# A two-layer hybrid decoder step: sample states by one product of three parts, conv states turned four at a time, and four smaller edits

## The chip, the cores and the metric

The kernel runs on one core of a Trainium2 chip. The metric is device time in microseconds (us); the time before is the median of 3 runs. The core has four engines that compute, each with its own queue: TensorE (PE in the profile, with its weight loads as PEld), VectorE (DVE), ScalarE (ACT) and GpSimd (POOL). SyncE (SP) issues the DMA transfers. PE's results go to PSUM, which has eight banks of 512 fp32 columns; everything else works from SBUF.

## The reference

One inference step of two layers, run for a prompt (512 tokens) and for 8 sample sequences of 8 new tokens, 576 tokens in all, with shared weights and a model width of 1024. Layer 0 has a pooling mixer (trailing means over 2, 4, 8 and 16 positions), layer 1 a gated DeltaNet mixer; each is followed by a SwiGLU FFN of width 2816, with an RMS norm before and after each part:

```
for i in range(DEPTH):
    h = rms_norm(x, norm_mix_pre[i])
    m = pool_mixer(h, ...) if i % 2 == 0 else gdn_mixer(h, ...)
    x = x + rms_norm(m, norm_mix_post[i])
    h = rms_norm(x, norm_ffn_pre[i])
    x = x + rms_norm(swiglu(h, ffn_w_in[i], ffn_w_out[i]), norm_ffn_post[i])
```

The DeltaNet mixer projects to q, k (8 heads of 128), v and a gate z (16 heads of 128), runs a causal convolution of width 4 over q, k and v, and then a recurrence per head on a state S of 128 x 128: S_t = a_t S_{t-1} + k_t (beta_t (v_t - a_t S_{t-1}^T k_t))^T, with output S_t^T q_t. The reference does it in chunks. Inputs and outputs also hold states: the last 15 pooling rows, the last 3 rows before the convolution (for each sample sequence and for the prompt, 4096 channels), and S itself for each sample sequence and head.

## The kernel before

**Numbers.** Operands of the large products are split into a rounded part and a remainder in a fast fp32 form (F32R): `split2` (line 1002) and `Weights.split` (981) make them with one ACT copy and one subtraction on DVE or POOL. `mm3` (990) then makes three products of each block: high x high, high x low, low x high. Small products are in plain fp32, and each of those leaves two records in the trace.

**Stages.** Activations lie with channels on partitions and tokens along columns, in two halves of 256 and 320 tokens (`HALVES`; the second holds the 64 sample tokens). First the pooling mixer and layer 0's FFN (lines 1224 to 1405), then the DeltaNet layer in four groups of two key heads and four value heads (`project`, `core`, `zgate`, lines 1523 to 2104), then the rest of its output product, and layer 1's FFN (2107 to 2199).

**FFN.** `ffn` (1098) has 22 column blocks, each a pair of a gate block and an up block. The first `head` pairs (`HEADS` = 7 in layer 0, 5 in layer 1, line 33) are made by `plain` (1125): for each half of the tokens it loads both weights and makes 24 products each, first all pairs of the first half, then all of the second. The others are made by `seven` (1144), which makes seven products of quarter blocks, of 288 columns each, in place of eight; it needs combinations of the weights (four half-size additions and subtractions on DVE or POOL) and of the activations (`twist`, 1085), and so both halves of the tokens.

**Norms.** `add_sq` (1011) squares each of the eight channel blocks on ACT and adds them into `nacc`, all but the last, which stays apart as a second addend `nsq`. `rstd` (1032) then sums over partitions by products of one column with a vector of ones, one for each addend and each 128 tokens; `finish1` (2177) does the same at the very end.

**Conv states.** `project` loads the 24 rows of earlier states (8 sequences x 3) as `crow`, 24 x 4 x 128, and turns each 128 channels by a transpose on PE (1548 to 1556); at the end (1652 to 1662) it turns the new rows `nct` back, 27 x 128 at a time (8 x 3 and the prompt's 3), copies them with ACT and stores them.

**Sample states.** `sample_front` (1694) prepares the keys of the 64 sample tokens: `ks` holds the rounded keys in rows 0 to 63 and their remainders in rows 64 to 127. `sample_heads` (1758) runs for each key head while the prompt's `scan` (1826) goes on. It loads the states of the 8 sequences, spreads `ks` into `km`, one block per sequence in which the other sequences' rows are zero, and updates each state by two products in one sum, with `vH` (the rounded values, in both row halves) and with `vL` (their remainders):

```
for bb in range(2):
    PE.matmul(pS[:, bb], km[:, b + bb], vH, start=True, stop=False)
    PE.matmul(pS[:, bb], km[:, b + bb], vL, start=False, stop=True)
```

Two smaller products per head use 64 rows of the array: `Ts` with `rs` (1794) and `Qs` with `vn` (1804, at a tile position).

**Order.** Nothing is issued as it is written. `Plan` (336) records all instructions, with costs per engine (`cost`, 434) and with the dependencies between them, and places them by a model of the engines (`forward`, 640). What is ready on an engine goes by rank; the table `MOVES` (line 53, 1405 entries) is a list of seeds that stir the ranks of stretches of instructions, one after the other. An instruction put on `EITHER` goes to DVE or POOL, one on `BOTH` to DVE or ACT, whichever the planner finds; where PE would stand idle long enough, it puts in products that nobody reads (`ps_w`). Buffers are rings of fixed size: three raw weight blocks, three split ones, and PSUM banks by name ("s": banks 0 to 2, "k": 6 and 5, "x": 7, `RING`, line 908).

Of the kernel before, what the change touches and what calls it, by code (L numbers as in the profile page):

```python
# [32 lines left out]
HEADS = (7, 5)  # L33
# [20 lines left out]
1.1d7anak.0.rf.u7 1.y2f47l.2s.0.bvc 1.s0vq82.2s.0.ti 1.pp743b.0.0.bvc 1.4z4ke2.0.9qg.a1k 0.au7bb7.2s.7t9.bo5  # L54
0.1frtbjm.2s.5sa.5v2 0.ee6mun.rs.39q.4fe 0.7sepyh.2bc.7i2.7t6 0.bbjoxv.rs.913.93v 0.8wxv3b.rs.3y7.40z
0.tf6kvk.rs.8tp.8wh 0.wyvqlx.2s.2to.3zc 0.bh9a6p.2bc.7q0.814 0.8hwl7j.2bc.816.8ca 0.jlysq9.8c.31x.47l
0.1nsdy99.8c.4iq.4tu 0.9yytj2.rs.27i.2im 0.igs0if.rs.9vd.b11 0.jxqs1k.rs.9jq.9uu 0.vegd0o.2s.0.3c0
0.1b0k30b.8c.9t0.9vs 0.pjwnuj.8c.hp.st 0.1643rle.rs.9wv.9zn 0.1urop5.2bc.73d.765 0.19ues0m.2bc.als.aok
0.67m20i.8c.71r.7cv 0.llkt9y.rs.6jb.6m3 0.bvvr7t.rs.7t7.84b 0.1q3ehmt.8c.23s.2ew 0.1qgeil4.2s.9ce.ai2
0.y8xkqt.8c.8x7.a2v 0.aoy0ng.rs.2pu.2sm 0.1fkb0ee.2bc.4c5.4ex 0.t07ml0.2bc.bmg.bvc 0.1xjj1qh.2s.9uj.9xb  # L60
0.1uf81p2.8c.6az.6dr 0.1d8z5m7.rs.2ch.2nl 0.1nsjl6j.2s.8kv.8vz 0.15jg0om.rs.89w.8co 0.hs4389.rs.anj.aqb
0.171qk9e.rs.7z4.81w 0.1140n12.2s.8hs.9ng 0.1azm7gz.2s.3ax.3m1 0.vijnsy.2bc.bss.bvc 0.10hprob.rs.1me.2s2
0.wi7odi.8c.89w.8co 0.dfvamo.2bc.aqa.at2 0.3jc2jj.8c.2e2.2gu 0.ps4ghp.2bc.56q.5hu 0.1r0ffal.2bc.8ya.912
0.xfacbh.2s.781.8dp 0.1fp5dk3.2bc.3ok.3zo 0.1slwoeh.2bc.70z.86n 0.1vgjcmy.2s.82h.985 0.1gi4m9f.2bc.4hm.4ke
0.87h1q0.rs.54h.5fl 0.rfnq0w.8c.8ql.bvc 0.q4hmzs.8c.9sc.a3g 0.10nufsc.2s.0.1q5 0.1tiapdn.2s.b6l.bvc
0.17t45od.rs.4a9.855 0.5rdedg.rs.9tc.9w4 0.1j4zh0k.2bc.6e.96 0.1ss67k0.rs.a6f.ahj 0.2svvgn.8c.agj.ajb
0.bpoomp.rs.bpu.bsm 0.t3o181.2bc.41f.4cj 0.1wv9twd.2s.1ck.57g 0.1tf1mpa.8c.od.1u1 0.69rvzm.2bc.9fe.9qi
0.1pj35r4.rs.9r8.9u0 0.1ce0uqr.8c.2um.40a 0.gjfyk0.8c.0.6p 0.46rblf.2s.3gc.3rg 0.14ty5f3.2s.8u9.9zx
# [12 lines left out]
0.a7ikvn.2s.6mv.6pn 0.1bygjfd.2s.bnt.bvc 0.1koaur1.rs.8pn.90r 0.1wf7dro.rs.98t.9jx 0.ji5ev1.rs.a90.ak4
0.1yp3jqj.rs.bfn.bif 0.1jv2yn6.rs.5vg.5y8 0.1mws14w.8c.8bp.9hd 0.i1evgw.2s.4gk.4jc 0.e2qeak.2bc.bb5.bm9
0.11gd8un.rs.92n.95f 0.1favvlm.8c.1fj.1ib 1.3ktxmq.0.7cu.7fm 0.177ynii.rs.9pq.ave 0.1r5eqxe.8c.33t.3ex
0.ma35m2.rs.1d5.2it 0.lymuvx.8c.2td.34h 0.1x8yzja.2s.a8.454 0.muxcdo.8c.8sl.8vd 0.14uzngk.2s.5gn.6mb
0.n0a1h5.8c.3t.3yp 0.1vmszuc.2s.36d.3hh 0.1kk9pm2.rs.7dk.7oo 0.17owqc0.2s.b0l.bvc 0.1cw9cxp.2bc.9n4.9y8
0.elx6d7.8c.5in.6ob 0.1dkpzq2.2bc.86x.89p 0.9mpa4v.8c.5dp.5ot 0.jijbp0.2bc.b6h.bhl 0.x120r.2s.7cw.8ik
0.2qokrq.rs.9ax.agl 0.ap74jx.rs.50w.5c0 0.1qf2ph5.rs.7w9.7z1 0.w56vte.rs.7ba.7e2 0.msgyjb.rs.6yq.84e
0.psozk2.2bc.8p9.8s1 0.6ru0ma.2bc.aag.alk 0.1ilo347.2s.8nn.bvc 0.yqg8b1.2s.a62.a8u 0.1mz5fg.8c.9ek.ak8
0.6lrs3y.8c.37r.3iv 0.4ffzsh.2s.9u8.a5c 0.kn8378.2bc.7w5.879 0.12kjhdl.rs.brk.buc 0.1gh7g5c.2s.7xy.892
0.18rvxdw.2s.5kq.5vu 0.1o2vxzq.2s.abg.bh4 0.17lajt1.2s.37i.3im 0.wyvpxk.8c.ss.13w 0.3czbgp.8c.4gk.4ro  # L90
0.1qng8px.2s.9wc.9z4 0.sobty9.2s.ahw.bvc 0.bi7va.2bc.335.3e9 0.1djjjua.2s.8rp.92t 0.1bvnacn.8c.vx.21l
0.171wwzd.8c.6ju.6uy 0.14u3rt5.rs.aqt.b1x 0.q50eg2.8c.9c7.ahv 0.vs1jfk.8c.bo5.bvc 0.1e1loh1.rs.7e1.7p5
0.1tmmbse.2s.9cm.9fe 0.nnoxbq.2s.b8o.bvc 0.n6n6h.2s.b8l.bvc 0.1o8bli5.8c.a52.a7u 0.bqy70q.2bc.b6l.bhp
0.isq8m3.rs.9ih.ao5 0.1274coh.2s.7is.8og 0.1b57b2j.8c.9m6.9xa 0.16oa8wk.2s.8ka.8n2 0.3w8q6h.rs.asp.b3t
0.1jutx9e.rs.b00.bb4 0.2zogkx.8c.6xh.709 0.1yuo622.rs.9pl.a0p 0.1ub0xk.2s.7ok.7zo 0.tki80c.2bc.7as.7dk
0.1ipjkno.2s.6sf.7y3 0.vhdfhd.rs.beg.bvc 0.mjbrxi.2bc.bcc.bf4 0.106vtjh.2bc.bjk.bmc 0.vomtm9.rs.9t3.a47
0.gggz5r.rs.bd9.bg1 0.v2xi33.8c.6n0.6y4 0.f42swr.2bc.70f.863 0.1qq27nd.8c.9ks.aqg 0.j464d9.rs.7w7.87b
0.1yozlmv.8c.bhg.bsk 0.5ntm1d.2bc.7cp.7nt 0.udmov4.2bc.8ug.8x8 0.ojoyjb.8c.9p9.aux 0.frz7ky.8c.7lc.7o4
0.l8y1qd.2s.98o.aec 0.ihecg0.8c.bef.bvc 0.1xadojx.2s.b7f.bvc 0.191175k.8c.agp.art 0.1u1nu8d.2s.60b.9v7
0.190c9ra.2s.581.6dp 0.ta4nji.rs.7pk.7sc 0.1hwnhjy.8c.aog.ar8 0.1nyltl2.2bc.5bk.5ec 0.1grqjg2.2s.9v6.b0u  # L100
0.3itv7y.8c.3lk.3oc 0.18rqmv.2bc.3k7.3mz 0.1i3b1pf.2bc.8ym.91e 0.h5wypn.2bc.bid.bl5 0.16uivga.8c.1gv.2mj
0.116d6uj.8c.aoc.azg 0.18ki0vc.2bc.bp0.brs 0.1es7bvt.rs.bse.bvc 0.2byfdo.8c.b7i.bim 0.4fyhs.2bc.bnt.bvc
0.h4jgec.8c.7ch.7nl 0.nhn8vl.2s.6yu.84i 0.1tp9pgh.2bc.858.8gc 0.18enz4u.2s.bab.bvc 0.1sg6l91.rs.bga.bvc
0.1hqzskx.rs.9ya.b3y 0.s3xg4v.8c.7o7.7qz 0.asw9he.2s.9d6.9oa 0.pvi32f.rs.9h3.9jv 0.1s43nou.8c.5h.89 0.zwcxin.2s.0.236
# [231 lines left out]
class Plan:  # L336
# [303 lines left out]
    def forward(self, rank):  # L640
# [65 lines left out]
        while todo:  # L706
# [1525 lines left out]
```

## Time and profile before

| what | before |
|---|---|
| time, median of 3 runs | 1530.03 us (1528.61 to 1533.35) |
| profiled execution, its time | 1528.16 us |
| its span, first to last instruction | 1526.4 us |
| PE busy | 1505.5 us (99%), 11856 records |
| PE weight loads busy | 1454.6 us (95%) |
| DVE busy | 1152.9 us (76%) |
| ACT busy | 835.7 us (55%) |
| POOL busy | 116.8 us (8%) |
| DMA | 198.91 MB, mean 130 GB/s |

Nearly all instructions stand at one line of the kernel (582, where the plan issues them), so groups are read by their tiles: "ps_s<-vL,km" is a product into a bank of ring "s" with `km` as weights and `vL` moving. Records of products overlap, since PE starts one before the last has left the array; a group's mean duration is therefore longer than the spacing between its products. Three DVE operations and more stand at lines 812 and 817, ACT's at 826, 829 and 835: these are the ones that the planner chose between the two engines.

### The profile page before, as it was taken

The numbers are of one execution on the slowest core, as the hardware profiler recorded it, in microseconds if no ns is written. First come the engines' busy times: TensorE is split into PE (matmuls) and PEld (weight loads), VectorE is DVE, ScalarE is ACT, GpSimd is POOL, SyncE is SP. The second block draws the span as 40 slices with busy tenths as digits, with TensorE's granted clock in tenths as the row PEclk, the third lists the DMA queues.
The fourth block names the chain that finished last, engine by engine and source line by source line (L and its number), as shares of the span: only waits on it lengthen the run. The fifth ranks groups of instructions, "written<-read, shape, count | busy, mean of one in ns | idle before, by whom it ended". The sixth has DMA issues, their size and how long they took to land. (4 is left out here: it accounts for less than half of the span.)

```text
span 1526.4 us, 30360 instructions
## 1 busy us (share of the span) xinstructions
PE 1505.5 (99%) x11856; PEld 1454.6 (95%) x11856; DVE 1152.9 (76%) x2323; ACT 835.7 (55%) x1765; POOL 116.8 (8%) x259
## 2 busy tenths in 40 slices
PE   8999999999999999999999999999999999999998
PEld 7999999999999999899899889989999999999998
DVE  5996358658788698997898799567799637837865
ACT  7764334324465975874874784746565334414455
POOL 4210000000012010110120010100110000000000
PEclk9999999999999999999999999999999999999999
DMA  6364323322476433434533443666865432332363
GB/s 190 110 188 138 99 82 97 99 82 84 135 224 184 130 103 100 113 103 123 145 100 102 126 123 111 199 177 190 244 207 157 113 88 66 94 101 70 102 190 124
DMA packets 350358, 198.91 MB, mean 130 GB/s; under 512 B 13963, under 2 KB 344364, under 8 KB 350207
## 3 DMA queue, kind: packets, MB, share of 16 engines
q1 hardware_dynamic: 350215, 196.97, 45.0%
q8 instruction: 93, 1.52, 0.4%
q14 instruction: 50, 0.41, 0.1%
HBM read 166.65 MB, written 30.52 MB: 129 GB/s over the span
## 5 line engine op out<-in xcount | busy, mean ns | idle before, releaser
L582 DVE TENSOR_TENSOR wl<-wraw,wh 128x1024 fp32r<-128x1024 f32 (+1 forms) x224 | 267.1, 1200 | 103.2 <-ACT wh L582 75.2
L582 ACT ACTIVATE wh<-wraw 128x1024 fp32r<-128x1024 f32 (+1 forms) x227 | 232.4, 1030 | 195.6 <-PE ps_A L582 70.7
L582 PE MATMUL ps_m<-hH,wh 128*128 128x256 f32 (+1 forms) x832 | 246.4, 309 | 0.0
L582 PE MATMUL ps_m<-hL,wh 128*128 128x320 f32 (+1 forms) x832 | 246.4, 308 | 0.0
L582 PE MATMUL ps_m<-hH,wl 128*128 128x256 f32 (+1 forms) x832 | 244.9, 307 | 0.0
L582 PEld LDWEIGHTS ps_m<-hH,wh 128*128 128x128 f32 x832 | 154.3, 189 | 2.8 <-issue 0.6
L582 PEld LDWEIGHTS ps_m<-hL,wh 128*128 128x128 f32 x832 | 154.6, 189 | 2.5 <-issue 0.5
L582 PEld LDWEIGHTS ps_m<-hH,wl 128*128 128x128 f32 x832 | 154.3, 190 | 2.4 <-issue 0.6
L582 PE MATMUL ps_B<-hH,wh 128*128 128x320 f32 (+1 forms) x392 | 114.8, 304 | 0.0
L582 PE MATMUL ps_B<-hL,wh 128*128 128x320 f32 (+1 forms) x392 | 114.0, 305 | 0.0
L582 PE MATMUL ps_B<-hH,wl 128*128 128x320 f32 (+1 forms) x392 | 113.2, 305 | 0.0
L582 PE MATMUL ps_B<-aH,wh 128*128 128x320 f32 x352 | 105.5, 311 | 0.6 <-ACT wh L582 0.6
L582 PE MATMUL ps_B<-aH,wl 128*128 128x320 f32 x352 | 105.8, 312 | 0.0
L582 PE MATMUL ps_A<-hH,wh 128*128 128x256 f32 (+1 forms) x376 | 104.7, 290 | 0.1
L582 PE MATMUL ps_B<-aL,wh 128*128 128x320 f32 x352 | 104.7, 310 | 0.0
L582 PE MATMUL ps_A<-hL,wh 128*128 128x256 f32 (+1 forms) x376 | 104.3, 288 | 0.0
L582 PE MATMUL ps_A<-hH,wl 128*128 128x256 f32 (+1 forms) x376 | 103.0, 288 | 0.0
L582 PE MATMUL ps_A<-aH,wl 128*128 128x256 f32 x352 | 94.6, 281 | 0.0
L582 PE MATMUL ps_A<-aL,wh 128*128 128x256 f32 x352 | 94.6, 281 | 0.0
L582 PE MATMUL ps_A<-aH,wh 128*128 128x256 f32 x352 | 94.4, 282 | 0.0
L582 DVE SCALAR_TENSOR_TENSOR ac<-u,cwt,ac 128x600 f32<-128x600 f32 x96 | 79.9, 844 | 2.5 <-ACT ac L582 2.1
L582 PEld LDWEIGHTS ps_B<-hH,wh 128*128 128x128 f32 x392 | 72.7, 188 | 0.1
(462 smaller groups left out, 4175.9 us busy)
## 6 DMA issues: line engine op xcount, KB each, us to landing
wraw<-in_ffn_w_in_dram SPq DMA_DIRECT2D x112, 512.0 KB
wraw<-in_gdn_w_in_dram SPq DMA_DIRECT2D x56, 512.0 KB
wraw<-in_ffn_w_out_dram SPq DMA_DIRECT2D x48, 448.0 KB
wraw<-in_gdn_w_out_dram SPq DMA_DIRECT2D x24, 512.0 KB
wraw<-in_ffn_w_out_dram SPq DMA_DIRECT2D x16, 512.0 KB
St<-in_state_gdn_rec_dram SPq DMA_DIRECT2D x32, 256.0 KB
out_dram<-St SPq DMA_DIRECT2D x32, 256.0 KB
z_d<-zz SPq DMA_DIRECT2D x16, 288.0 KB
```

The costliest lines, as they stand in the source:

```text
L582: calls[e](*a, **k)
```

## The change

- Layer 0's FFN has 6 plain pairs in place of 7; one more pair is made by `seven`.
- Sample states: four sequences' tokens are 32 rows. `ks` and `vHL` are laid out so that one product of 128 rows holds three parts of 32 rows each, rounded keys with rounded values, rounded keys with the values' remainders, and the keys' remainders with rounded values; the fourth quarter is zero. There are two such layouts, for sequences 0 to 3 and 4 to 7. The remainders' own product, which was in the sum before, is left out. `km` is made in two halves with a new mask, `seqm4`.
- The products with `Ts` and `Qs` run over all 128 rows, with zeros (memsets on POOL) in the rows that don't count; `vn` is needed in the upper rows alone and may go to DVE or ACT.
- Conv states are loaded and stored with four channel blocks under each other on partitions (96 rows in, 108 out), so that one transpose turns four; each block has its own transfers.
- `add_sq` adds the last square to the sum, except in layer 0's mixer norms (`apart`).
- The planner's model: a POOL copy costs 137 ns more; an instruction on an engine other than PE that touches a PSUM bank waits in the model for the bank's last user on another engine than PE; and `MOVES` is a new table of 574 entries.

```
-HEADS = (7, 5)
+HEADS = (6, 5)
...
-                t = 0.85 * n + (100 if method == "memset" else 183)
+                t = 0.85 * n + (100 if method == "memset" else 320)
...
+            late = max((quiet[x] + self.LAT[e] - t for x in ops[i][10] if user.get(x, e) not in (e, "PE")), default=0.0)
+            if e != "PE" and late > 0.0:
+                hold, done = hold + late, done + late
...
-            if c == NC - 1:
+            if c == NC - 1 and apart:
                 acc.append(sq)
...
-                crow = pp.tile([R0, 4, P], F32, name="crow", tag="nco", bufs=1)
+                crow = pp.tile([4 * R0, P], F32, name="crow", tag="nco", bufs=1)
                 for j, i0, n in pc:
...
-                for j in range(4):
-                    PE.transpose(cp[:, 4 * j4 + j], crow[:, j], ident[:R0, :R0])
-            ACT.activation(cst_t.rearrange("p c b r -> p c (b r)"), cp, AF.Copy)
+                    for i in range(n):
+                        SP.dma_start(crow[(j + i) * R0:(j + i + 1) * R0],
+                                     state_gdn_conv[0].rearrange("b r d -> (b r) d")[:, (i0 + i) * P:(i0 + i + 1) * P])
+                PE.transpose(cp[:, 4 * j4 * R0:4 * (j4 + 1) * R0], crow, ident[:4 * R0, :4 * R0])
+            ACT.activation(cst_t.rearrange("p c b r -> p (c b r)"), cp, AF.Copy)
...
-                for j in range(4):
-                    PE.transpose(pn_[:R, j], nct[:, 4 * j4 + j], ident)
-                ACT.activation(nco, pn_[:R], AF.Copy)
+                nco = pp.tile([4 * R, P], F32, name="nco", tag="nco", bufs=1)
+                pn_ = bank("x")[:4 * R, :P]
+                PE.transpose(pn_, nct[:, 4 * j4:4 * j4 + 4].rearrange("p c r -> p (c r)"), ident)
+                BOTH.move(nco, pn_)
...
-                ACT.activation(ks[:, hd], pt, AF.Copy)
-                DVE.tensor_tensor(ks[E2[1], hd], pt[E2[1]], ks[E2[1], hd].bitcast(F32), op=sub)
+                for x_ in range(2):
+                    BOTH.move(ks[:, hd, x_], pt)
+                for x_ in range(2):
+                    a, b, c = (slice(32 * q, 32 * q + 32) for q in (x_, 1 - x_, 2 + x_))
+                    BOTH.move(ks[b, hd, x_], pt[a])
+                    DVE.tensor_tensor(ks[c, hd, x_], pt[c], ks[c, hd, x_].bitcast(F32), op=sub)
...
-                EITHER.tensor_tensor(km, ks[:, hd:hd + 1].bitcast(F32).to_broadcast([P, NB, P]),
-                                   seqm2.unsqueeze(2).to_broadcast([P, NB, P]), op=mult)
+                for x_ in range(2):
+                    b4 = slice(4 * x_, 4 * x_ + 4)
+                    EITHER.tensor_tensor(km[:, b4], ks[:, hd, x_:x_ + 1].bitcast(F32).to_broadcast([P, 4, P]),
+                                         seqm4[:, b4].unsqueeze(2).to_broadcast([P, 4, P]), op=mult)
...
-                    PE.matmul(pv[:, 0, e * P:(e + 1) * P], Ts[:, hd, e], rs[:, e], start=True, stop=True)
...
+                    PE.matmul(pv[:, 0, e * P:(e + 1) * P], TQ[:, hd, e], sn[:, 0, e], start=True, stop=True)
+                BOTH.scaled(vn, pv[up, 0].rearrange("p (e v) -> p e v", e=2), bet[up, SPANS, h2])
...
-                split2(ve, vH, vL)
+                vHL = cp_.tile([P, 2, 2, P], F32R, name="vHL", tag="vHL", bufs=1)
+                for x_ in range(2):
+                    BOTH.move(vHL[:, x_], ve)
+                for x_ in range(2):
+                    a, b = (slice(32 * q, 32 * q + 32) for q in (x_, 1 - x_))
+                    EITHER.tensor_tensor(vHL[b, x_], ve[a], vHL[a, x_].bitcast(F32), op=sub)
...
-                    PE.matmul(po[up, 0, e * P:(e + 1) * P], Qs[:, hd, e], vn[up, e], start=True, stop=True,
-                              tile_position=(SMP, SMP))
+                    PE.matmul(po[:, 0, e * P:(e + 1) * P], TQ[:, hd, e], sn[:, 2, e], start=True, stop=True)
...
-                        PE.matmul(pS[:, bb], km[:, b + bb], vH, start=True, stop=False)
-                        PE.matmul(pS[:, bb], km[:, b + bb], vL, start=False, stop=True)
+                        PE.matmul(pS[:, bb], km[:, b + bb], vHL[:, b // 4], start=True, stop=True)
```

More of the change, by code (lines that the diff above doesn't have):

```diff
@@ L59 @@
[L59 to L68, printed above, removed]
@@ L656, in forward @@
         still = {name: len(h) for name, h in self.holds.items()}
-        quiet = {}
+        quiet, user = {}, {}
         def note(t, work):
@@ L782, in forward @@
                 quiet[name] = max(quiet.get(name, 0.0), end)
+                user[name] = e
             for j in succ[i]:
@@ L892, in hybrid_kernel @@
     seqm = seqm2[:SMP]
+    seqm4 = cst.tile([P, NB], F32, name="seqm4")
+    for q in range(4):
+        sm = seqm4[32 * q:32 * q + 32].rearrange("p (x b) -> p x b", x=2)
+        POOL.affine_select(sm, ones[:32, :NB].rearrange("p (x b) -> p x b", x=2), [[0, 2], [-NT, NB // 2]], ALU.is_ge, 0.0,
+                           base=0, channel_multiplier=1)
+        POOL.affine_select(sm, sm, [[0, 2], [NT, NB // 2]], ALU.is_ge, 0.0, base=NT - 1, channel_multiplier=-1)
+    POOL.memset(seqm4[64:96, 4:], 0.0)
+    POOL.memset(seqm4[96:, :4], 0.0)
     prm = cst.tile([P, 73], F32, name="prm")
@@ L1654, in project @@
             for j4, pc in enumerate(pieces):
-                nco = pp.tile([R, 4, P], F32, name="nco", tag="nco", bufs=1)
-                pn_ = bank("x", (P, 4, P))
-                for j in range(4):
-                    PE.transpose(pn_[:R, j], nct[:, 4 * j4 + j], ident)
-                ACT.activation(nco, pn_[:R], AF.Copy)
+                nco = pp.tile([4 * R, P], F32, name="nco", tag="nco", bufs=1)
+                pn_ = bank("x")[:4 * R, :P]
+                PE.transpose(pn_, nct[:, 4 * j4:4 * j4 + 4].rearrange("p c r -> p (c r)"), ident)
+                BOTH.move(nco, pn_)
                 for j, i0, n in pc:
-                    src = nco[:, j:j + n].rearrange("r c p -> r (c p)")
-                    SP.dma_start(nc_prompt[0, 0, :, i0 * P:(i0 + n) * P], src[:CW - 1])
-                    SP.dma_start(nc_sample[0].rearrange("b r d -> (b r) d")[:, i0 * P:(i0 + n) * P], src[CW - 1:])
+                    for i in range(n):
+                        src, cols = nco[(j + i) * R:(j + i + 1) * R], slice((i0 + i) * P, (i0 + i + 1) * P)
+                        SP.dma_start(nc_prompt[0, 0, :, cols], src[:CW - 1])
+                        SP.dma_start(nc_sample[0].rearrange("b r d -> (b r) d")[:, cols], src[CW - 1:])
         def zproj(h):
@@ L1898, in core @@
             TQ = cp_.tile([P, 2, 2, P], F32, name="TQ", tag="TQ", bufs=1)
-            Ts, Qs = TQ[:SMP], TQ[SMP:, :, :, :SMP]
-            ks = cp_.tile([P, 2, P], F32R, name="ks", tag="ks", bufs=1)
+            Ts, Qs = TQ[:SMP], TQ[SMP:, :, :, SMP:]
+            POOL.memset(TQ[SMP:, :, :, :SMP], 0.0)
+            ks = cp_.tile([P, 2, 2, P], F32R, name="ks", tag="ks", bufs=1)
             Uv = Uw.rearrange("p (h s) i -> p h s i", h=4)
```

413 lines of the change are left out of this document (126 added, 287 removed).

## The prediction

> **What bounds the kernel now.** I read the page's busy times and slices first, then busy time by stage, then the chain of waits for what one product costs, and last the tiles that the change touches.
>
> ```profile
> span 1526.4 us, 30360 instructions
> PE 1505.5 (99%) x11856; PEld 1454.6 (95%) x11856; DVE 1152.9 (76%) x2323; ACT 835.7 (55%) x1765; POOL 116.8 (8%) x259
> PE   8999999999999999999999999999999999999998
> ```
>
> PE has no hole that a slice of 38 us shows. But products overlap in the trace, so a busy PE says only that something was in flight. By stage (columns: us, then PE, PE's weight loads, DVE, ACT, POOL busy, each with its count; the middle row is the DeltaNet stage):
>
> ```profile
> 0.00:500.00 500.00, 494.01 (x3695) 486.46 (x3696) 356.50 (x633) 247.23 (x430) 45.30 (x108) 1.00 0.46 131
> 500.00:1055.00 555.00, 546.40 (x4653) 505.70 (x4653) 462.00 (x1146) 370.15 (x981) 58.18 (x138) 1.00 0.45 128
> 1055.00:1526.00 471.00, 465.10 (x3512) 462.44 (x3510) 334.35 (x546) 218.30 (x356) 13.35 (x13) 1.00 0.46 133
> ```
>
> In all three stages PE's idle time is small (6, 8.6 and 5.9 us) and its clock is full. So the time is, to first order, the sum of what PE issues; a product taken out shortens the run by its spacing to the next, not by its duration. The spacing stands in the chain of waits, where runs of one kind follow each other (start, us, tile, records):
>
> ```profile
> 1058.96 17.46 PE ps_A L582 x144
> 1087.27 11.73 PE ps_B L582 x80
> 1446.12 4.26 PE ps_A L582 x32
> 1111.64 1.01 PE ps_n L582 x10
> ```
>
> The first is output products of 256 columns: 17.46/144 = 0.121 us each. The second, of 320: 0.147. The third, a seven-product pair with 288 columns: 0.133. The fourth, the norm's sums over partitions, one column wide in plain fp32: 0.101 a record, and an fp32 product leaves two records. Width hardly helps there.
>
> **The change part by part: PE.**
>
> ```profile
> L582 PE MATMUL ps_s<-vL,km 128*128 128x256 f32 x64 | 17.3, 289 | 0.3 <-DVE vL L582 0.3
> L582 PE MATMUL ps_n<-ones,nsq 128*128 128x1 f32 x68 | 11.8, 243 | 0.0
> L582 PE MATMUL ps_x<-ident,nct 128*27 128x128 f32 x32 | 5.0, 272 | 0.0
> L582 PE MATMUL ps_x<-ident,crow 24*128 24x24 f32 x32 | 3.4, 220 | 0.0
> 577.70 0.27 PE L582 MATMUL ps_x<-ident,nct 128*27 128x128 f32 x1
> 962.04 0.60 PE L582 MATMUL ps_x<-ident,nct 128*27 128x128 f32 x4
> 500.96 0.42 PE L582 MATMUL ps_x<-ident,crow 24*128 24x24 f32 x4
> 992.32 0.71 PE L582 MATMUL ps_s<-sn,TQ 64*128 64x128 f32 x4
> 996.97 0.65 PE L582 MATMUL ps_s<-sn,TQ 64*64 64x128 f32 x4
> ```
>
> *Sample states.* The second product per sequence (vL) goes: 64 x 0.121 = 7.8 us. *Conv states.* Outgoing turns fall from 32 to 8; four take 0.60 and one 0.27, so (0.60 - 0.27)/3 = 0.11 each: 24 x 0.11 = 2.6. Incoming ones fall from 32 of 24 columns, (0.42 - 0.21)/3 = 0.07 each (0.220 is the duration of one), to 8 of 96 columns. That form is not in the trace; it lies between 0.07 and 0.11, so the gain is 2.2 less 0.6 to 0.9: I take 1.5. *Last square.* The norms with two addends are ten half-norms that now have one (after layer 0's FFN both norms, after the layer 1 mixer both, and the last): 25 products, 50 records x 0.101 = 5.0. Layer 0's mixer norms keep two. *Plain pairs.* One pair costs 48 x 0.121 + 48 x 0.147 = 12.9 us, a seven-product pair 84 x 0.133 = 11.2: gain 1.7. *Ts and Qs products over all rows.* Four records take 0.71 and 0.65 where four full-height records (nct) take 0.60; 8 x (0.11 + 0.05) = 1.3 is the upper end, 0 the lower (the full form of a product, not a turn, is not shown here; no row gives a loss). I take 1.0.
>
> PE's sum: 7.8 + 2.6 + 1.5 + 5.0 + 1.7 + 1.0 = 19.6 us, of which 12.9 in the DeltaNet stage.
>
> **ACT, DVE, POOL.**
>
> ```profile
> L582 ACT ACTIVATE ks<-ps_k 128x128 fp32r<-128x128 f32 x8 | 2.2, 281 | 0.6 <-PE ps_m L582 0.3 <-PE ps_k L582 0.2
> L582 DVE TENSOR_TENSOR ks<-ps_k,ks 64x128 fp32r<-64x128 f32 x8 | 2.4, 294 | 0.7 <-ACT ks L582 0.6
> L582 DVE TENSOR_TENSOR km<-ks,seqm 128x1024 fp32r<-128x1024 f32 x8 | 9.8, 1222 | 5.6 <-PE ps_k L582 5.6
> L582 DVE TENSOR_TENSOR wraw<-wraw,ws 128x512 f32<-128x512 f32 x32 | 22.0, 688 | 0.3
> L582 DVE TENSOR_TENSOR vL<-sn,vH 128x256 fp32r<-128x256 f32 x8 | 3.4, 421 | 0.0
> L582 ACT ACTIVATE vH<-sn 128x256 fp32r<-128x256 f32 x8 | 3.3, 415 | 2.5 <-DVE sn L812 2.4
> L582 ACT ACTIVATE nco<-ps_x 27x512 f32<-27x512 f32 x8 | 4.7, 586 | 7.7 <-DMA out_dram<-nco 4.4 <-PE ps_x L582 3.3
> ```
>
> Eight times (two per head group): ks grows from one copy and one subtraction to four copies and two subtractions, 3 x 281 + 294 = 1.14 us; a 32-row form is not shown, and since the time goes by columns in the row of 64 rows (294) as in that of 128 (281), I take the same. km becomes two halves: 2 x 688 - 1222 = 0.15. vH and vL become two copies and two subtractions: 415 + 421 = 0.84. Together 8 x 2.13 = 17.0, less eight copies of nco that shrink from 512 to 128 columns, 8 x (586 - 281) = 2.4: 14.6 us more for DVE and ACT. In the DeltaNet stage these have 555 - 462 = 93 and 555 - 370 = 185 us free, so on average it hides. It does not everywhere:
>
> ```profile
> 550.00:575.00 25.00, 24.50 (x187) 23.24 (x186) 24.48 (x63) 15.17 (x32) 0.91 (x6) 1.00 0.39 111
> 675.00:700.00 25.00, 23.00 (x177) 22.71 (x176) 23.60 (x68) 13.62 (x28) 0.63 (x5) 1.00 0.28 81
> 900.00:925.00 25.00, 23.30 (x175) 21.99 (x174) 24.56 (x62) 16.76 (x37) 3.66 (x7) 1.00 0.23 64
> ```
>
> In such slices DVE is full and PE already waits; the ks copies fall next to them. So of the 12.9 us saved in this stage I count three quarters, 9.7 (ends: 0 and 12.9). The quarter is my choice, not a row. The memsets are POOL's, with 497 of 555 us free there.
>
> *Pair and cover.* The new seven-product pair costs DVE four 688 ns steps and more, but at 120 to 160 us there is room (row of 150:200 below). What the lost plain pair covered is nearer: the second half's activations.
>
> ```profile
> 98.92 0.49 DVE L582 TENSOR_TENSOR hL<-y,hH 128x320 fp32r<-128x320 f32 x1
> 105.21 0.28 PE L582 MATMUL ps_A<-hH,wl 128*128 128x256 f32 x1
> L582 DVE TENSOR_TENSOR tL<-y,tH x8: 754/758/760, 109.7 to 119.4; 128x576 fp32r<-128x576 f32 x8
> L582 PE MATMUL ps_B<-tH,wh x24: 292/295/298, 149.9 to 251.8; 128*128 128x288 f32 x24
> 150.00:200.00 50.00, 50.00 (x377) 49.88 (x376) 19.00 (x24) 15.82 (x26) 0.00 (x0) 1.00 0.33 96
> ```
>
> The first half's plain pairs end at 105.5; one fewer ends 48 x 0.121 = 5.8 us earlier, 99.7. The second half's last activation is there at 99.4. It just meets, at no cost; with the cover gone it would cost up to 5.8. The twist is done at 120.1, the first seven-product pair moves from 149.9 to about 137: 17 us to spare.
>
> *DMA queue.* Per group, loads of conv states go from 3 to 8 and stores from 6 to 16: 60 more issues in all.
>
> ```profile
> L582 SPq DMA_DIRECT2D out_dram<-nco x24: 257/290/1225, 579.0 to 970.7; - x24
> L582 SPq DMA_DIRECT2D crow<-in_state_gdn_conv_dram x12: 309/322/394, 489.4 to 851.5; - x12
> SPq L582 <- DVE wl L582: 326.5, 101, 14.8
> ```
>
> 40 x 0.29 + 20 x 0.32 = 18 us of SP's time, at most 8 x 0.29 = 2.3 us in one burst, ahead of weight loads. SP waits 326.5 us for weight buffers to be freed alone, so it is early, and I price this at nothing; uncovered it is 18.
>
> *The end.* The last square's add lies on the last chain:
>
> ```profile
> 1518.44 0.40 ACT nsq L582
> 1519.32 0.80 ACT gy L582 x2
> ```
>
> One DVE add of 256 columns (vL's 0.42) against four records less (0.4), while ACT works on gy until 1520.1 anyway: between -0.4 and +0.6, I take +0.2.
>
> **Order and bank rule.** The planner gets a wait between engines on one PSUM bank and a dearer POOL copy. The trace has such waits:
>
> ```profile
> DVE vn L812 <- ACT ve L829: 8.9, 8, 3.2
> ```
>
> Both only read the same products, yet one stands behind the other, 8.9 us in 8 cases, and the old planner did not know. An order made with it can gain; one made of 574 moves in place of 1405 can lose. I take 0. The bank of ks is now read by four copies and two subtractions, one behind another where ACT and DVE share them: 1.14 us longer, 8 times, 9.1 us if the next user of the bank always stands waiting.
> The Trainium skill, "PSUM — Partial Sum Buffer", section "PSUM bank collisions raise a hardware error", says that two engines may not touch one bank and quadrant at once, reads included, and that the compiler's scheduler therefore puts a dependency between them. The vn row agrees, and by that rule the 9.1 us are a possible loss that speaks against this change.
>
> **The sum.** Outside the DeltaNet stage 5.0 + 1.7 = 6.7, inside 9.7, the end +0.2: -16.2 us. The profiled execution took 1528.16 us (its span and 1.8 around it): 1512.0. The median of the runs is 1.9 above it: 1514.
>
> **The rivals.**
> *The order itself pays (0.15).* All of the 12.9 comes (3.2 more) and half of the stage's 8.6 us of PE idle goes: 1506. For: the 8.9 us of vn. Against: DVE's full slices.
> *The cover falls short (0.10).* PE waits for the second half at about 100 us, 5.8: 1520. For: DVE is full there, and 99.4 against 99.7 is no margin. Against: a pair less is also two weight splits less for DVE ahead of it.
> *Bank of ks (0.08).* The 9.1 us come onto the path: 1523. Against: PE has projection products to do meanwhile.
> *The products were hidden, so the change doesn't do what it says (0.06).* Nothing of the 12.9 comes: 1524. For: the waits in slices with DVE full. Against: 546.4 of 555.
> *The order loses (0.05).* PE idles three times as long in the stage, 17 us more: 1531; the slice 675:700 at its worst loses 2.0 of 25, which over the stage would be 44.
> *Slower: vector work sets the stage (0.06).* One mechanism, from 500 to 1055 us: DVE and ACT, not PE, pace the heads, so none of the 12.9 comes and the whole 14.6 is added. 1530.0 - 6.7 + 0.2 + 14.6 = 1538. It decides once DVE is busy above 24.5 of 25 us in most slices, as now in 900:925. Against: 462 of 555 over the stage.
>
> **How the numbers follow.** The forecast has 0.50; its own range is 1509 to 1519 (the quarter either way, the ends of turns, end and Ts/Qs). A measurement here tells about 0.3% (4.6 us) from no change, so faster means under 1525.4. Faster: 0.50 + 0.15 + 0.10 + 0.08 + 0.06, less 0.03 that lies near the bound: 0.86. Same: the losing order and that 0.03: 0.08. Slower: 0.06. The range of 8 in 10 takes in the rivals up to 1528 and down to 1504.
>
> **What would show it.** In the profile after: 11682 PE records and the fillers' difference; 64 products of km, 20 of the 68 nsq records, 8 and 8 turns; the DeltaNet stage some 10 us shorter with DVE about 470 us busy; the first product with tH near 137; PE without a hole at 98 to 106. Wrong if PE's busy share in that stage falls under 97%, or if the stage is as long as before although the products are gone.

## The result and the profile after

The changed kernel is slower: 1537.28 us (median of 22 runs, 1531.49 to 1551.34) against 1530.60 for the kernel before (22 runs, 1527.87 to 1534.29). The ratio is 1.005, its 95% interval 1.0036 to 1.0065. Forecast were 1514 us and a range of 1504 to 1528. The profiled execution took 1533.3 us, 5.1 more than that of before.

The page after (totals), then its busy time by stage, with the columns as before (the middle row is the DeltaNet stage):

```profile
span 1531.6 us, 30346 instructions
PE 1497.5 (98%) x11740; PEld 1447.8 (95%) x11740; DVE 1166.2 (76%) x2379; ACT 843.3 (55%) x1794; POOL 128.0 (8%) x284
```
```profile
0.00:500.00 500.00, 492.57 (x3681) 484.77 (x3682) 362.73 (x643) 246.85 (x432) 48.03 (x120) 1.00 0.45 129
500.00:1055.00 555.00, 535.88 (x4547) 498.15 (x4545) 465.91 (x1183) 375.59 (x1006) 68.57 (x152) 0.99 0.45 127
1055.00:1526.00 471.00, 468.99 (x3517) 464.89 (x3515) 335.14 (x553) 220.83 (x357) 11.39 (x12) 1.00 0.45 132
```

PE has 116 records less and is busy 8.0 us less, and the span is 5.2 us longer. In the DeltaNet stage PE was idle 8.6 of 555 us; now it is idle 19.1. Part of what is issued is fillers, the products that nobody reads; before, then after:

```profile
L578 PE MATMUL ps_w<-ones x62: 270/275/580, 1.3 to 1496.3; 128*128 128x128 f32 x62
```
```profile
L411 PE MATMUL ps_w<-ones x120: 270/275/582, 1.3 to 1523.9; 128*128 128x128 f32 x120
```

A row further down has 16 of them in 1.95 us, 0.122 each, so the 58 more are some 7 us of PE, an estimate. No run left them out: whether they cost time, or only stand where PE would wait, is open. The groups of PE by tile, after (count, duration in ns, first and last start in us):

```profile
L415 PE MATMUL ps_e<-hH,wh x64: 277/283/388, 459.8 to 489.6; 128*128 128x256 f32 x64
...
L415 PE MATMUL ps_s<-vHL,km x64: 274/282/469, 630.7 to 1054.4; 128*128 128x256 f32 x64
...
L415 PE MATMUL ps_n<-ones,nsq x20: 166/250/250, 34.9 to 85.8; 128*128 128x1 f32 x20
...
L415 PE MATMUL ps_x<-ident,nct x8: 270/272/321, 577.4 to 974.6; 128*108 128x128 f32 x8
...
L415 PE MATMUL ps_A<-tH,wh x8: 288/295/297, 136.8 to 152.1; 128*128 128x288 f32 x8
```

The same groups of the kernel before:

```profile
L582 PE MATMUL ps_e<-hH,wh x64: 278/283/364, 460.1 to 490.3; 128*128 128x256 f32 x64
...
L582 PE MATMUL ps_s<-vL,km x64: 274/282/468, 625.7 to 1050.8; 128*128 128x256 f32 x64
```

So the products went as forecast, and the time did not. The first product of ring "e" and the last with `km` cut the span in three: up to the DeltaNet layer 460.1 us before and 459.8 after; from there to the last sample state 590.7 and 594.6; behind it 475.6 and 477.2. The first part gained 0.3 us, the last lost 1.6, and in the middle 3.9 were lost where 9.7 were to be won.

Of the new waits, two places are shown here. The first, with the longest, is the conv rows. PE and the DMA queue, after (SPq is the queue's own issue; then windows):

```profile
583.02 2.47 SPq L415 DMA_DIRECT2D out_dram<-nco  x7
...
586.78 1.54 SPq L415 DMA_DIRECT2D crow<-in_state_gdn_conv_dram  x4
...
590.20 0.30 PE L415 MATMUL ps_x<-ident,crow 96*128 96x96 f32 x1 [3.79 <-DMA crow<-in_state_gdn_conv_dram]
```
```profile
580.00:590.00 10.00, 6.41 (x50) 6.21 (x48) 8.62 (x26) 2.42 (x6) 0.00 (x0) 1.00 0.31 77
590.00:600.00 10.00, 9.80 (x61) 9.80 (x62) 2.70 (x12) 2.05 (x5) 0.00 (x0) 0.83 0.21 60
```

Loaded and turned-back rows share one buffer, so the next group's four loads go out only behind the stores of the last, and PE stands 3.79 us for them. Then its clock falls: in the next 10 us it was granted 0.83 on the mean, that is half clock for about 3.4 us, some 1.7 us of work lost. The Trainium skill, "TensorE: Matmul & The Clock Gate", section "Part 1: The HAM clock gate (the "warmup" mystery)", says that an idle window of about 3.4 us halves the clock and a busy one restores it; this trace agrees here, with 3.79 us idle and then about 3.4 us at half clock.

The second is the norm ahead of layer 1's FFN. DVE before (the last addition into `nacc`, then the first step behind the sums), then DVE after, then PE after:

```profile
1130.83 0.48 DVE L582 TENSOR_TENSOR nacc<-nacc,nsq 128x320 f32<-128x320 f32 x1
...
1133.84 0.16 DVE L582 TENSOR_SCALAR nv<-ps_n 128x3 f32<-128x3 f32 x1
```
```profile
1131.12 0.48 DVE L415 TENSOR_TENSOR nacc<-nacc,nsq 128x320 f32<-128x320 f32 x1
...
1132.65 0.48 DVE L415 TENSOR_TENSOR nacc<-nacc,nsq 128x320 f32<-128x320 f32 x1
...
1133.39 0.48 DVE L415 TENSOR_TENSOR nacc<-nacc,nsq 128x320 f32<-128x320 f32 x1
...
1135.46 0.15 DVE L415 TENSOR_SCALAR nv<-ps_n 128x3 f32<-128x3 f32 x1
```
```profile
1131.42 1.95 PE L411 MATMUL ps_w<-ones 128*128 128x128 f32 x16
1133.93 0.83 PE L415 MATMUL ps_n<-ones,nacc 128*128 128x1 f32 x6 [0.57 <-DVE nacc L415]
1135.14 0.39 PE L415 MATMUL ps_A<-hH,wh 128*128 128x256 f32 x1 [0.39 <-ACT sg L415]
```

The additions end 2.6 us later than before (1133.39 against 1130.83), and PE has run out of other work by 1131.4: it makes fillers, which nobody reads, and waits.

The granted clock varied more from run to run after (0.985 to 0.997) than it does for the kernel before (0.994 to 0.999). In the profiled execution of the changed kernel, apart from the first 25 us and the last 5, it stands at half in three stretches of 3.4 us (the third number from the end is the clock):

```profile
590.50:593.90 3.40, 3.40 (x15) 3.40 (x14) 0.00 (x0) 0.00 (x0) 0.00 (x0) 0.51 0.38 108
754.40:757.80 3.40, 3.40 (x13) 2.08 (x12) 2.57 (x9) 2.90 (x12) 0.43 (x3) 0.50 0.52 147
1136.70:1140.10 3.40, 3.40 (x19) 3.40 (x18) 2.40 (x14) 0.00 (x0) 0.00 (x0) 0.50 0.85 248
```

At half clock each does the work of 1.7 us, so they cost some 5.1 us, an estimate, and the two profiled executions differ by 5.1; that of the kernel before has no such stretch between 15 and 1522 us. The table below therefore gives, next to the median, the median of time x clock, an estimate of the time less what the clock took. By it the changed kernel has 1528.1 us and the one before 1524.6 to 1525.7: about half of the loss of the median is clock and half is not.

### The profile page after: what moved, and what is told of

Its sections match the earlier page's. It is cut to its first block, busy times and chain, and to the rows that moved or that the text cites. A ratio compares the mean times of both kernels' runs of the same rounds, so it can differ in the third digit from the quotient of the medians.

```text
span 1531.6 us, 30346 instructions
## 1 busy us (share of the span) xinstructions
PE 1497.5 (98%) x11740; PEld 1447.8 (95%) x11740; DVE 1166.2 (76%) x2379; ACT 843.3 (55%) x1794; POOL 128.0 (8%) x284
## 5 line engine op out<-in xcount | busy, mean ns | idle before, releaser
L415 DVE TENSOR_TENSOR wl<-wraw,wh 128x1024 fp32r<-128x1024 f32 (+1 forms) x222 | 263.1, 1190 | 93.3 <-ACT wh L415 45.3
L415 PE MATMUL ps_m<-hH,wh 128*128 128x256 f32 (+1 forms) x832 | 250.0, 312 | 1.3 <-ACT u L415 1.0
L415 PE MATMUL ps_B<-hH,wh 128*128 128x320 f32 (+1 forms) x376 | 109.8, 306 | 0.4 <-ACT sg L415 0.4
L415 PE MATMUL ps_B<-hL,wh 128*128 128x320 f32 (+1 forms) x376 | 108.7, 304 | 0.0
L415 PE MATMUL ps_B<-hH,wl 128*128 128x320 f32 (+1 forms) x376 | 108.3, 304 | 0.1
L415 ACT ACTIVATE aH<-sg 128x576 fp32r<-128x576 f32 (+2 forms) x55 | 32.3, 587 | 72.3 <-DVE sg L415 72.3
```

The costliest lines, as they stand in the source:

```text
L415: calls[e](*a, **k)
```

## The experiments

Every edit of this kernel makes the planner choose another order for everything. To change one thing at a time, the experiments take the order from a list, either that of the kernel before ("old order") or of the changed one ("new order"):

```diff
-        for move in MOVES.split():
...
-        best = self.forward(rank)
+        best = 0, plan
```

Instructions that an edit adds or changes are placed by their dependencies and, where stated, by the planner's times; all others keep engine and place. Times are medians; the difference is to the kernel before on the same chip.

| run | median us | difference | ratio, 95% interval | time x clock |
|---|---|---|---|---|
| changed kernel | 1537.28 | +6.7 | 1.0036 to 1.0065 | 1528.1 |
| e1 squares undone, new order | 1543.85 | +13.6 | 1.0057 to 1.0118 | 1529.1 |
| e2 conv buffers, new order | 1534.34 | +4.1 | 1.0011 to 1.0039 | 1524.8 |
| e3 both | 1531.55 | +1.3 | 0.9997 to 1.0024 | 1524.1 |
| e4 old work, new order | 1544.16 | +13.9 | 1.0071 to 1.0100 | 1535.0 |
| e5 squares alone, old order | 1536.45 | +6.2 | 1.0031 to 1.0056 | 1528.4 |
| e6 conv alone, old order | 1544.04 | +13.8 | 1.0077 to 1.0106 | 1534.6 |
| e7 conv with buffers, old order | 1542.87 | +12.6 | 1.0069 to 1.0095 | 1537.4 |
| e8 sample alone, old order | 1549.03 | +18.8 | 1.0109 to 1.0135 | 1537.7 |
| e9, e17, e18 controls, old order | 1535.60, 1534.27, 1532.60 | +4.6, +3.2, +1.6 | 1.0016 to 1.0037, 1.0013 to 1.0037, 0.9998 to 1.0021 | 1529.8, 1527.8, 1528.2 |
| e10 control, new order | 1546.62 | +15.6 | 1.0086 to 1.0119 | 1534.2 |
| e11 sample undone, new order | 1539.55 | +8.6 | 1.0039 to 1.0065 | 1531.1 |
| e12 conv undone, new order | 1532.08 | +1.1 | 1.0001 to 1.0020 | 1526.1 |
| e13 products out, old order | 1528.24 | -2.1 | 0.9978 to 0.9997 | 1522.4 |
| e14 products in, new order | 1538.11 | +7.7 | 1.0038 to 1.0063 | 1529.6 |
| e15 new stage in the old order | 1535.43 | +5.1 | 1.0023 to 1.0048 | 1528.5 |
| e16 conv and squares undone, new order | 1534.69 | +4.3 | 1.0018 to 1.0041 | 1529.4 |

### Are the products the path? (e13, e14)

```diff
-                        PE.matmul(pS[:, bb], km[:, b + bb], vH, start=True, stop=False)
-                        PE.matmul(pS[:, bb], km[:, b + bb], vL, start=False, stop=True)
+                        PE.matmul(pS[:, bb], km[:, b + bb], vH, start=True, stop=True)
```

> The kernel before, with the 64 products of the sample states' small part (km by vL) left out and nothing else touched; the split that makes vL stays. So the states miss that small part. Its 64 records stood 0.121 us apart each, 7.8 us. If TensorE's products set the stage's end, as the prediction took it: -5.9 (three quarters) to -7.8, 1522 to 1525 us. If the chain of waits sets it (the spared products come back as idle time): -2 at the most, 1528 to 1531 us.

Measured: -2.1 us (the interval is -3.4 to -0.5; by time x clock -2.6). This is the cleanest of the runs: no vector work, no instruction placed anew. The stage (columns as before) in the kernel before and then in this run:

```profile
500.00:1050.00 550.00, 541.40 (x4617) 500.70 (x4617) 457.55 (x1137) 366.45 (x972) 58.18 (x138) 1.00 0.45 127
```
```profile
500.00:1050.00 550.00, 541.06 (x4561) 496.47 (x4560) 458.30 (x1139) 366.62 (x974) 58.68 (x138) 1.00 0.45 127
...
L549 PE MATMUL ps_s<-vH,km x64: 277/282/468, 624.7 to 1049.2; 128*128 128x256 f32 x64
```

PE has 56 records less in these 550 us and is busy as long as before, 541 us. The row that the forecast leaned on can't tell work from slack: records overlap (282 ns long, 121 apart), so a product that comes a little later still touches the one before. Of 7.8 us of products about 2 were on the path. The rest turned into spacing that the busy time doesn't show.

The other direction, in the changed kernel:

```diff
                         PE.matmul(pS[:, bb], km[:, b + bb], vHL[:, b // 4], start=True, stop=True)
+                        PE.matmul(pS[:, bb], km[:, b + bb], vHL[:, b // 4], start=True, stop=True)
```

> The changed kernel, with each of its 64 km products issued twice in a row (the second writes the same result over the first) and nothing else touched. If TensorE's products set the stage's end: +7 to +8, 1544 to 1545 us. If the chain of waits sets it: the products fill idle time, +1 to +3, 1538 to 1540 us (they also lengthen the chain of the sample states by 0.12 us each).

Measured: 1.0 us more than the changed kernel by the differences, 1.5 by time x clock. In its one profiled execution the stage was 5.0 us longer (462.4 to 1062.0), so the runs say less here than in the first, and the interval is nearly that of the changed kernel; all of it is under the 7 to 8 that products on the path would have cost.

### The order with the old work (e4) and the controls (e9, e10, e17, e18)

e4 is the kernel before with its table of moves replaced by the new order, and one pair less:

```diff
-HEADS = (7, 5)
+HEADS = (6, 5)
```

> The kernel's work of before (sample states by two products, conv states one at a time, last square apart) in the order of the changed kernel, with its 6 plain pairs and its fillers; 210 of the instructions that the undone parts bring back or touch were placed anew so that the planner's own times show no new wait; by these times the order is as good for the old work (1492 us) as the old order was (1491). Theory of the waits (order neutral, edits lose): 1528 to 1533 us, as the kernel before. Theory of the order (the edits gain their 18 us, the order loses 25): 1550 to 1556 us.

Measured: +13.9, of which the expectation for a neutral order had none. Its stage, and the rows that cut its span:

```profile
500.00:1060.00 560.00, 550.99 (x4666) 509.37 (x4667) 458.01 (x1147) 373.60 (x983) 67.46 (x131) 1.00 0.45 126
...
L554 PE MATMUL ps_e<-hH,wh x64: 278/283/384, 462.9 to 494.0; 128*128 128x256 f32 x64
...
L554 PE MATMUL ps_s<-vL,km x64: 274/282/468, 633.8 to 1062.1; 128*128 128x256 f32 x64
...
1140.45 1.95 PE L550 MATMUL ps_w<-ones 128*128 128x128 f32 x16
...
1144.71 0.38 PE L554 MATMUL ps_n<-ones,nacc 128*128 128x1 f32 x2 [2.31 <-DVE nacc L554]
```

PE is busy 98.4% of the stage, as before, and yet the stage takes 599.2 us for 590.7. And the norm ahead of layer 1's FFN waits here too (fillers, then 2.31 us for `nacc`) although the last square is apart in this kernel: that wait belongs to the order first, and not to the addition alone. The new order also brings its 120 fillers along.

But e4 has 235 instructions that follow another one on their engine than in the new order. The controls ask what that costs by itself. They have no edit:

> A control: the kernel before with no edit at all. 120 instructions of its DeltaNet stage were put up to 30 places earlier or later in the written-out order (about 3 us), so that 264 instructions of 15384 follow another one on their engine, and kept only where the planner's own time stayed the same (1491.3 us both). If placing anew costs nothing by itself, as the three theories so far take it: 1530 us, within 0.2%. Theory of the tuned place (the old order is the best on the chip of many that the planner's times can't tell apart, so that any other place of 200 instructions loses, edit or not): 1536 to 1546 us, and the runs in which 195 to 235 instructions were placed anew say little of their edits.

> The control again with another random draw: the kernel before with no edit, 224 instructions of its DeltaNet stage follow another one on their engine, the planner's time the same (1491.1 against 1491.3 us). If the first control shows the size of it: 1534 to 1537 us, and the 13 us of the runs with as many instructions placed anew are more than placing. If the first control was a lucky draw: 1540 us and more, and those 13 us can't be told from it.

> The control with a third random draw: 280 instructions follow another one on their engine, the planner's time the same (1491.4 us). As for the second control: 1534 to 1537 us if the first one shows the size of it, 1540 us and more if that was a lucky draw.

> The same control on the changed kernel: no edit, 120 instructions of its DeltaNet stage put up to 30 places away, 302 instructions then follow another one on their engine, the planner's time within 0.9 us. If placing anew costs nothing: 1537 us. Theory of the tuned place: the changed kernel's order would be such a pick too, 1543 to 1553 us; if it is no better than its neighbours on the chip (the planner's times chose it alone), 1532 to 1542 us.

Measured: +4.6, +3.2 and +1.6 in the old order; in the new one 8.9 more than the changed kernel. Placing 224 to 302 instructions anew, at nearly the same time by the planner, came out slower in all four draws, in the smallest (e18) not clear of nothing. So of e4's 13.9 the order itself would have 5 (by the control in the new order) to 12 (by the smallest one in the old). That is an estimate from four random draws, and the fillers and the pair less are in it. The planner's times, which were 12.6 us lower for the changed kernel than for the one before (each by its own model), do not order such versions.

### The parts, each undone in the new order (e1, e2, e3, e11, e12, e16)

e1 takes the last addition back, at all places:

```diff
-            if c == NC - 1 and apart:
+            if c == NC - 1:
                 acc.append(sq)
```

> The changed kernel with one part undone: the last square of every sum goes to TensorE again as a product of its own (25 products back, 10 additions gone). Every other instruction keeps the engine and the place in the order that it has in the changed kernel. Theory of the waits (the edits do the sparing that was forecast, but the last addition now stands on the chain of a sum of squares at the ends of the stages): 25 products at 0.10 to 0.20 us come back, +2.5 to +5 us, and the idle time that the trace after shows newly at the two boundaries and in the tail (2.7 at 450-475 us, 6.3 at 1125-1175, some 2.5 after 1475) goes, -11.5: about 1530 us, 0.5% under the changed kernel. Theory of the order (the new order loses by itself) and theory of the sample chain (its vector work and waits lose): only the products come back: 1540 to 1542 us.

Measured: 6.9 us more than the changed kernel, where a gain of 6 or a loss of 3 to 5 was expected. Nearly all of it is clock: time x clock differs by 1.0. Its clock was 0.987 in half of its runs.

e2 leaves the squares and mends the conv rows:

```diff
-                crow = pp.tile([4 * R0, P], F32, name="crow", tag="nco", bufs=1)
+                crow = pp.tile([4 * R0, P], F32, name="crow", tag="crow", bufs=2)
```

> The changed kernel with the conv rows that are loaded given two buffers of their own, so that they no longer wait until the turned rows of the group before have landed in DRAM; their loads are issued 12 us ahead of the turn by the planner's times instead of some 3 us. All else as in the changed kernel. Theory of the waits: TensorE's idle 3.8 us at 586 us goes and with it the 3.4 us at half clock behind it (1.7), and the same at 754 us: -7 to -10, about 1528 us. Theory of the order, theory of the sample chain: the next wait takes its place, 1535 to 1538 us.

> The two edits before this one together: squares apart again, and conv rows in buffers of their own and loaded 12 us ahead. Theory of the waits: the two places lie apart, so the gains add: 1521 to 1524 us, faster than the kernel before. Theory of the order, theory of the sample chain: 1538 to 1542 us.

Measured: e2 2.6 us under the changed kernel, e3 5.4. The wait is gone in both traces (no idle time of PE that ends at a load of `crow`), and by time x clock e2 gains 3.3, nearly the 3.79 us of the wait. e3 stands level with the kernel before. So the conv rows are one shown cause, worth about 3 us, although the intervals of e2 and the changed kernel touch.

e12 undoes the conv part whole, e11 the sample part, e16 conv and squares (the old lines come back):

```diff
-                PE.transpose(cp[:, 4 * j4 * R0:4 * (j4 + 1) * R0], crow, ident[:4 * R0, :4 * R0])
+                for j in range(4):
+                    PE.transpose(cp[:, 4 * j4 + j], crow[:, j], ident[:R0, :R0])
```

> The changed kernel with one part undone: conv states turned one at a time again, with the loads and stores as before. All else as in the changed kernel; 215 of the other instructions follow another one on their engine; by the planner's times 4.9 us more. As the prediction had the term (4.1 us of turns): 1541 us. Theory of the waits (late conv loads cost 7 to 10 us and the clock window behind them): 1531 to 1534 us. Theory of the tuned place: 1543 us and more, whatever the part is worth.

> The changed kernel with one part undone: sample states by two products again, so that 64 km products and the split come back and the copies and differences of three parts go. All else as in the changed kernel; 80 of the other instructions follow another one on their engine than there; by the planner's times 5.1 us more. As the prediction had the term (7.8 us of products, 1.0 of others): 1543.5 to 1546 us. Theory of the sample chain (the vector work and waits of this part lose more than its products save): 1530 to 1534 us.

> The changed kernel with two parts undone, the conv states (as in the run with that part alone) and the last square; what is left of the change is the sample states' one product, 6 plain pairs and the new order. No instruction but the returned ones is placed otherwise than in the run with the conv states undone (1532.1 us). Theory of the waits: the additions leave the boundaries, as with the conv buffers (-2.8 from one run to the next there): 1528 to 1530 us. If the squares are worth their products, as the prediction had it: 1535 to 1537 us.

Measured: without the conv part 5.6 us less than the changed kernel, although 215 instructions were placed anew; the part, forecast at +4.1 of gain, costs 5.6 by the medians and 2.0 by time x clock, both before anything that this placing cost. Without the sample part 1.9 us more by the medians, but the intervals nearly coincide: no loss by that part is shown, and no clear gain; a quarter of the 7.8 that its products stood for, as e13 has it, would fit. With the squares undone as well, e16 is 3.2 above e12, where e3 is 2.8 under e2. By time x clock, undoing the squares costs 1.0 (e1) and 3.3 (e16) and gains 0.7 (e3). So in the new order the sign of the squares' part is not settled, and a gain of 5.0 is not shown.

### The parts, each alone in the old order (e5 to e8)

> The kernel before with one part of the change alone: the last square is added to its sum (25 products of the square tile gone, 10 additions more). All else, the order too, as before. As the prediction had it (25 products of two records at 0.101 us each, gone from TensorE's path): -5, about 1525.5 us. Theory of the waits (the addition stands on the chain at the ends of the stages): the sum's end comes later by an addition and a wait, some 1 to 1.5 us at each of five places: 1531 to 1536 us. Theory of the order (edits gain, only the new order loses): 1525.5 us, as the prediction.

e5 is the squares' part alone (the line of e1 the other way, the order untouched but for nine instructions). Measured: +6.2, by time x clock +3.4. DVE and then PE ahead of layer 1's FFN in this run:

```profile
1131.84 0.49 DVE L549 TENSOR_TENSOR nacc<-nacc,nsq 128x320 f32<-128x320 f32 x1
1132.24 1.22 DVE L549 TENSOR_TENSOR wl<-wraw,wh 128x1024 fp32r<-128x1024 f32 x1
1133.38 0.48 DVE L549 TENSOR_TENSOR nacc<-nacc,nsq 128x320 f32<-128x320 f32 x1
...
1135.25 0.15 DVE L549 TENSOR_SCALAR nv<-ps_n 128x3 f32<-128x3 f32 x1
```
```profile
1133.92 0.38 PE L549 MATMUL ps_n<-ones,nacc 128*128 128x1 f32 x2 [0.99 <-DVE nacc L549]
```

The last addition comes at 1133.38, with a weight subtraction of 1.22 us between it and the one ahead of it. PE waits 0.99 us for it, and the norm's next step starts at 1135.25; in the kernel before it was 1133.84. The products taken out had lain in front of the norm's end, beside other work; the addition lies on it in this trace. This execution was the fastest of the six (1530.88 us), and the place shows 1.4 us of later start; where the rest of the 6.2 lies was not found.

> The kernel before with one part of the change alone: conv states turned four at a time, with the loads and stores cut into four each, loads and turned rows in one shared buffer. Order as before; of the instructions of this part 113 were placed by the planner's times so that they show no new wait. As the prediction had it (2.6 + 1.5 us of turns gone): 1526.5 us. Theory of the waits (the loads, each behind the stores of the group before, land late): 1529 to 1536 us, with TensorE waiting for the conv rows. Theory of the order: 1526.5 us.

> The run before this one with the loaded conv rows in two buffers of their own and their loads issued 12 us ahead of the turn. Theory of the waits: the wait for the rows is gone and the 4.1 us of turns show: 1526 to 1527 us. As the prediction and the theory of the order have it: 1526.5 us, no different from the run before it.

> The kernel before with one part of the change alone: sample states by one product of three parts, with its moves, differences and full-height products. Order as before; 99 of the instructions that this part touches were placed by the planner's times, which still show 2.5 us more than for the kernel before, because the copies of three parts come late for the products behind them. As the prediction had it (64 products of 0.121 us and 1.0 us of other products gone, three quarters of it counted): about 1523.5 us; the whole of it: 1521.5. Theory of the waits, theory of the sample chain: 1528 to 1534 us. Theory of the order: 1521.5 to 1523.5 us.

Measured: +13.8, +12.6 and +18.8. These three have 136 to 195 instructions placed anew, so part of it is placing (1.6 to 4.6 by the controls in this order); the rest exceeds these draws, and no part is seen to pay in the old order. What they don't show is why: in e7 the wait for `crow` (1.8 us of PE in e6) is gone and the time is 1.2 us under e6, so in the old order the late rows are not the main cause. That stays open.

### The new stage between old ends (e15)

> The kernel before, with the DeltaNet stage of the run with both repairs (sample states by one product, conv states four at a time with buffers of their own) in that run's order, and outside the stage the old work (7 plain pairs, last square apart) in the old order; at the two joins 290 instructions were placed by the planner's times, which give 1485.9 us against 1491.3 for the kernel before. If the loss lies in the new order at the start, the boundaries and the tail (2, 3, 3 to 6 and 1 to 2 us more idle time than before), and the stage is as long as before: 1528 to 1532 us with the clock as for the kernel before. If the stage itself gains once the rest is undisturbed: 1522 to 1526 us. Theory of the tuned place (joins placed anew cost): 1535 us and more.

Measured: +5.1. The stage didn't gain with the rest as before (463.1 to 1059.2, 596.1 us); what the 290 instructions placed anew at the joins cost can't be told apart in it. No version with all of the work beat the kernel before; e3 and e12 come within 1.3 us of it.

## Why the prediction was wrong

**The step that failed first** is "the time is, to first order, the sum of what PE issues; a product taken out shortens the run by its spacing". The prediction had said itself that a busy PE "says only that something was in flight", and then took 546.4 busy of 555 as proof against the rival that the products were hidden. e13 measured that rival: 64 products of 7.8 us gave 2.1. The quarter held back from the stage's 12.9 should have been some three quarters, if the other products there are hidden as these are. Both signs of being wrong that the prediction had named came: PE is busy 96.6% of the stage (535.88 of 555), and the stage is no shorter (594.6 us for 590.7). What sets the stage's end in PE's place was not found; the many short waits for DVE there, none over 2 us before, are a guess.

**Counts.** Right: 11740 records are the 11682 forecast plus 58 records of fillers; 64 km products, 20 of nsq, 8 turns out; the first product with tH at 136.8 (forecast 137), no hole of PE at 100 us. DVE's 465.9 us in the stage are near the 470. So the work was forecast well and its worth was not.

**Clock, taken as full.** The forecast has no term for it. By time x clock 3 to 4 of the 6.7 us are clock; the stretch at half clock from 590.5 us follows the wait for the conv rows.

**Last square, 5.0, counted in full.** Alone in the old order it loses, +6.2 (e5); in the new order its sign is not settled. At the norm ahead of layer 1's FFN the edit put an addition on the path, where the sum waits for the last one, and the product that it took out was not on it. That place shows 1.4 of the 6.2.

**DMA issues at nothing**, hidden under SP's waits for weight buffers. Wrong: the wait was not for SP's time but for the one buffer that loads and stores share, 3.79 us of PE and a clock window behind it. Worth 3 us (e2).

**Order at nothing, its loss at 0.05.** Wrong: an estimated 5 to 12 of the 13.9 of e4. The rival had 17 us, by PE idling three times as long in the DeltaNet stage. In e4 that did not show: PE is idle 9.0 of 560 us there, as before, and part of the loss lies at the norm. What the 58 more fillers have in it is open.

**Vector work hidden.** Not contradicted: with the sample part undone the time rises by 1.9 (e11), which is not clear of nothing. The waits at the bank of ks, a rival at 9.1 us, did not come: PE waits 0.6 us for `ks`, before 0.9. The rival in which vector work sets the stage had 1538 us, near the 1537 measured, but that is luck: its sign, DVE busy above 24.5 of 25 us in most slices, came in 2 slices of 22 from 500 to 1050 us.

**One pair less, cover at 100 us.** No wait appeared. Its 1.7 us were not tried alone, and the start of the DeltaNet layer moved by 0.3 in all.

Hidden products and a losing order were taken as alternatives to each other; the runs have both. 1524 for the hidden products, 5.0 for the squares that did not come either, 3 for the conv rows and 5 for the order, its lower end, make 1537. That sum was made after the result and has no term of its own for the clock, so its fit proves nothing.

## What to carry to other kernels

Before counting a product as time, look at whether its engine has slack that the busy share hides: where records overlap, 98% busy held room for some 6 of 8 us of work. Taking such products out, or issuing them twice, with nothing else moved is a cheap test of that, and it can come ahead of the rewriting. In a kernel whose order is searched, an edit brings a new order with it, and that is a change of several us, here a loss in all four controls, that the search's own times don't rank; two or three controls that shuffle a few hundred instructions at equal planned time say how large it is.

## What the runs showed of the hardware

In these traces the clock also fell without a long idle stretch, and it stayed down under load. After the short waits at 1131 to 1135 us shown above (fillers, one-column sums, about 1 us idle in all), the changed kernel ran for 3.4 us at half clock:

```profile
1133.50:1137.00 3.50, 2.68 (x20) 2.60 (x21) 3.38 (x7) 1.75 (x3) 0.00 (x0) 0.95 0.80 224
1137.00:1140.20 3.20, 3.20 (x17) 3.20 (x17) 2.10 (x12) 0.00 (x0) 0.00 (x0) 0.52 0.86 252
```

And in e2 PE was busy all the time at half clock from 35 to 60 us. The first row lies ahead of it, with fillers, small fp32 products and one-column sums, and PE was never idle in it:

```profile
32.00:35.40 3.40, 3.40 (x28) 3.00 (x27) 2.42 (x6) 1.91 (x7) 0.00 (x0) 1.00 0.29 60
35.00:40.00 5.00, 5.00 (x20) 4.55 (x20) 1.74 (x6) 0.61 (x3) 0.28 (x1) 0.54 0.11 35
40.00:45.00 5.00, 5.00 (x23) 4.68 (x21) 3.60 (x9) 3.51 (x9) 2.70 (x4) 0.50 0.39 131
45.00:50.00 5.00, 5.00 (x21) 4.74 (x21) 3.73 (x12) 1.99 (x7) 0.00 (x0) 0.50 0.00 0
50.00:55.00 5.00, 5.00 (x24) 5.00 (x24) 1.82 (x4) 1.98 (x6) 0.00 (x0) 0.50 0.00 0
55.00:60.00 5.00, 5.00 (x21) 4.69 (x21) 1.88 (x7) 2.51 (x6) 0.00 (x0) 0.50 0.00 0
```

The same stretch of the changed kernel's profile:

```profile
45.00:50.00 5.00, 5.00 (x41) 4.72 (x40) 3.88 (x13) 3.47 (x10) 0.00 (x0) 1.00 0.00 0
```

21 products instead of 41 in 5 us, some 12 us lost over 25, with the same code and order at that place. The Trainium skill, "TensorE: Matmul & The Clock Gate", section "Part 1: The HAM clock gate (the "warmup" mystery)", gives for the clock's return at least one busy window of about 3.4 us. Here PE was busy for seven of them and stayed at half, so one is not always enough, and the measurement decides. Such a stretch is common in the new order. In eight of its ten profiled executions (the changed kernel's and nine runs') one begins between 34.5 and 37.1 us; it lasts 3.4 or 6.8 us in six of them and 27.3 in e1 and e2. In the kernel before no run had a mean clock under 0.994. What tips one execution into this and another not was not found.
